# Small tiles of an encoder kernel padded or moved in SBUF

## The chip, the cores and the metric

The kernel runs on one core of one Trainium2 chip. The metric is the time of one execution on the device in microseconds (us); a smaller time is better. TensorE multiplies matrices (its weight loads are listed apart, as PEld), VectorE (DVE) and ScalarE (ACT) do elementwise work, GpSimd (POOL) does a few small operations, and SyncE (SP) issues the transfers from HBM. A core's working memory, SBUF, has 128 partitions; a tile takes the same bytes in each of them, so its place is one byte address within a partition.

## The reference, cut to what matters

The input x has 256 tokens of 2048 float32 values. Two layers follow each other. Each computes `x = LN(alpha*x + mixer(x))` and then `x = LN(alpha*x + SwiGLU(x))`.

- Layer 0's mixer is one projection of 2048 to 8192 columns, which feeds neighbourhood attention (8 heads) and a bidirectional gated recurrence (8 heads); their outputs, 2048 columns, go through an output projection of 2048 to 2048.
- Layer 1's mixer is a projection of 2048 to 2560 columns, which feeds multi-scale pooling and grouped-query attention, and again an output projection of 2048 to 2048.
- SwiGLU is `(silu(x @ w_gate) * (x @ w_up)) @ w_down` with a hidden width of 5632.

All data are float32. Nearly all of the arithmetic is the product of 256 tokens with these weight matrices.

## The kernel before

**Products.** A weight matrix is cut into pieces of 256 rows by 512 columns. One transfer brings a piece into the tile `raw` (line 139). It is split into two tiles, `whi` (a copy rounded to the fast matmul type, ACT, line 102) and `wlo` (the rest, DVE, line 103), each 4096 bytes a partition. Activations are split the same way into `xTh`/`xTl` or `yTh`/`yTl`. `mm3` (line 239) then makes each product from three matmuls: (whi, low activation), (whi, high), (wlo, high). The activation is the stationary operand, 128 by 128, loaded by LDWEIGHTS; the weight tile is the moving operand, 128 by 512, which streams through. A piece is 12 such matmuls: 2 token tiles, 2 row blocks, 3 parts. There are 760 pieces, so 9120 matmuls of 512 columns, all recorded at line 242. The other matmuls (attention, recurrence, transposes) move 128 or 256 columns.

**Where weight pieces lie.** `load_half` (line 123) takes the split tiles from rings of buffers in turn: `wp` has 6 buffers for `whi` and 6 for `wlo`. After layer 0's mixer, line 809 opens a second ring `wx` with 2, and lines 811 and 819 a third one, `f0` or `f1`, with 3 (called fp below). A newly opened ring is left alone for 12 pieces; then the pieces go round all rings, with 11 slots while fp is open and 8 slots during layer 1's mixer. So until the first `wx` piece, the 1705th of the 512-column matmuls, only `wp` is read; of the 7416 from there on, 4200 read `wp`, 1368 `wx` and 1848 fp (counted in the program: the trace holds the program's 10,180 matmuls in the program's order, so each matmul of the trace is matched to its buffers).

**Addresses.** Pools are laid out one behind the other in the order in which they are opened: `cp` (two constants), `wp`, `acts` (activations), `sm` (small tiles), and behind them `ab` (layer 0's mixer), or `res`, `wx`, and `f0`, `cd` or `f1`. Small tiles are rounded up to 32 bytes. The program's own list of addresses gives:

| tiles | first address | address modulo 256 |
|---|---|---|
| `ident`, 512 bytes | 1152 | 128 |
| `mhalf`, 32 bytes | 1664 | 128 |
| `raw`, `whi`, `wlo` of `wp` (each 4096 bytes) | 1696 | 160 |
| `xTh`, `xTl`, `yTh`, `yTl` (65,536 bytes in all) | 67232 | 160 |
| `sm`: 1344 bytes of small tiles | 132768 | 160 |
| all of `ab`: `qT`, `kT`, `pt`, `av`, `qq`, `kk`, ... | 134112 | 224 |
| `whi`, `wlo` of `wx` | 150496 | 224 |
| `gam`, `bet` (8192 bytes each), `betT` (64 bytes) | 166880 | 224 |
| `whi`, `wlo` of fp, behind `betT` | 183328 | 32 |
| `cc`, `sn`, `nwq`, `nwk`, `pscale` (32 bytes) of `cd` | 166880 | 224 |
| `rcount` and all that follows in `cd`: `band`, `dv`, `dkT`, `dqT`, `pt`, `cn`, `pw`, ... | 169984 | 0 |

**Order of the work.** The framework plans the order of each engine's instructions from the program and its priorities; loads and splits run ahead of the products by up to as many pieces as there are buffers. SP's queue holds the weight transfers in program order.

**Lines of the change.** `ident` and `mhalf` (lines 83 to 86) are made once on POOL; `mhalf` is the exponent -0.5 of `rstd_of` (line 199). `mv` (line 263) holds mean and variance in `norm`. `betT` (line 329) is a bias that `flip` reads. `pscale` (line 681) scales the pooling output.

Of the kernel before, what the change touches and what calls it, by code (L numbers as in the profile page):

```python
# [11 lines left out]
F32 = mybir.dt.float32  # L12
# [4 lines left out]
PSUM = bass.MemoryType.PSUM  # L17

P = 128
T = 256  # L20
NT = T // P
D = 2048
KT = D // P
# [14 lines left out]

# column blocks (units of 128) of the chunks of the first projection
A_Q, A_K, A_V, H_Q, H_FF, H_FB, H_I, H_G = (8 * i for i in range(8))  # L40
# [32 lines left out]
def trunk(ctx: ExitStack, tc: tile.TileContext, a, out):  # L73
    nc = tc.nc
# [6 lines left out]
    ps = ctx.enter_context(tc.tile_pool(name="ps", bufs=1, space=PSUM))  # L81

    ident = cp.tile([P, P], F32, name="ident")
    make_identity(nc, ident)
    mhalf = cp.tile([P, 8], F32, name="mhalf")
    nc.gpsimd.memset(mhalf, -0.5)

# [1 line left out]
    def acc():  # L89
# [14 lines left out]

    # a norm whose transposes go between the next products, one step a piece
    pending = []

    # pools with room for split weight pieces, taken in turn
    rings = [(wp, 6)]
    turn = [0]  # L110

    def open_ring(pool, bufs):
        # the first pieces keep to the older pools: the new one's memory may still be in use
        rings.append((pool, bufs))
        turn[0] = -12

    # instructions that the splits of the next pieces are queued behind
    ahead = []
    held = [0]
    last_load = [None]  # L120
    first = [True]
# [27 lines left out]
    def mm_chunk(halves, lhs, outs, tok_major=False, after=None, before=None):  # L149
        """outs[tok] += x[tok] @ w for the chunk; halves: (dram piece, first k tile)."""  # L150
        n = len(halves)
        loaded = []

        def step():
            if next(pending[0], None) is None:
                pending.pop()

        def mms(i, tok, pin=False):
            hi, lo = loaded[i]
            k0 = halves[i][1]  # L160
            for kk in range(2):
                xh, xl = lhs(tok, k0 + kk)
                first = i == 0 and kk == 0
                last = i == n - 1 and kk == 1
                mm3(outs[tok], (xh, xl), (hi[:, kk, :], lo[:, kk, :]), first, last, pin)

        if tok_major:
            for i, (src, _) in enumerate(halves):
                if pending and i >= FREE:
                    held[0] = 1  # L170
                loaded.append(load_half(src))
            for tok in range(NT):
                for i in range(n):
                    if pending and i >= FIRST_STEP:
                        step()
                    mms(i, tok, True)
                    if pending and tok == 0:
                        held[0] = HELD
                while pending:
                    step()  # L180
                if after:
                    after(tok)
        else:
            for i, (src, _) in enumerate(halves):
                loaded.append(load_half(src, before(i) if before else ()))
                for tok in range(NT):
                    mms(i, tok)
            if after:
                for tok in range(NT):
                    after(tok)  # L190

    def rstd_of(var, n, scale=None, eps=LN_EPS):
        """(var * scale + eps) ** -0.5, [P, n]"""
        r = sm.tile([P, 8], F32, tag="rstd", name="rstd", bufs=6)
        if scale is None:
            nc.vector.tensor_scalar(r[:, :n], var, eps, None, op0=add)  # L196
        else:
            nc.vector.tensor_scalar(r[:, :n], var, scale, eps, op0=mult, op1=add)
        nc.gpsimd.tensor_tensor(r[:, :n], r[:, :n], mhalf[:, :n], op=ALU.pow)  # L199
        return r  # L200

    # activations of the current projection, transposed and split, per token tile
    def new_xT():
# [19 lines left out]

    # transposes of src [P tok, 512] into the group's token slice, split
    def transpose4(src, hi, lo):
# [13 lines left out]
    def mm3(o, lhs, rhs, start, stop, pin=False):  # L239
        """o += lhs.T @ rhs, both as high and low parts"""  # L240
        for n, (a, b) in enumerate(((1, 0), (0, 0), (0, 1))):
            ins = nc.tensor.matmul(o, lhs[a], rhs[b], start=start and n == 0, stop=stop and n == 2)  # L242
            if pin:
                tc.keep_in_program_order(ins)
# [3 lines left out]

# [1 line left out]
    def residual_tools(res, gam, bet, betT):  # L250
# [11 lines left out]
        def norm(tok, xT=None, out_rows=None):  # L262
            mv = sm.tile([P, 2], F32, tag="mv", name="mv")
            nc.vector.bn_aggr(mv, stats[tok])
# [59 lines left out]
    def load_gb(pool, i, which):  # L324
        g = pool.tile([P, D], F32, tag="gam", name="gam", bufs=1)
        b = pool.tile([P, D], F32, tag="bet", name="bet", bufs=1)
        nc.sync.dma_start(g, a[f"ln_{which}_g"][i : i + 1, :].to_broadcast([P, D]))
        nc.sync.dma_start(b, a[f"ln_{which}_b"][i : i + 1, :].to_broadcast([P, D]))
        bT = pool.tile([P, KT], F32, tag="betT", name="betT", bufs=1)
        nc.sync.dma_start(bT, a[f"ln_{which}_bT"][i])  # L330
        return g, b, bT

# [1 line left out]
    def out_proj(w, order, groups, res, gb):  # L334
# [15 lines left out]

# [1 line left out]
    def ffn(fp, layer, xT, res, gb, last):  # L352
# [41 lines left out]

# [1 line left out]
    def attend(pool, probs, v_of):  # L396
        """o [d, h, q] = (probs[h] [q, k] v [k, d]).T in PSUM, for two heads"""
        pts = []
# [12 lines left out]
    def exp_rows(pool, src, nm):  # L411
        """softmax of src [P, NT, T] with the negated row maxima nm"""
        e = pool.tile([P, NT, T], F32, tag="e", name="e", bufs=2)
# [9 lines left out]
    def ab_mixer(mp, xT, yT):  # L423
        def load_x(i):
            """the part of x that goes with piece i of the first chunk"""
            if i % 2:
# [20 lines left out]
        def constants_in():  # L447
            first[0] = False
            with tc.issue_after(last_load[0]):
# [3 lines left out]
                nc.sync.dma_start(colmask, a["col_mask"])  # L453
            # lower bounds: cumulative softmax over the layers' logits, less its first
            nc.vector.tensor_tensor(ex, lg, lg, op=sub)
# [6 lines left out]
        lhs = x_lhs(xT)  # L462
# [15 lines left out]
        def pairT(t, col):  # L478
            """two heads at column col of t [tok, 512] -> psum [d, 2, T]"""
            q = trp().rearrange("p (h t) -> p h t", h=2)  # L480
            for h in range(2):
                for tok in range(NT):
                    transpose(
                        q[:, h, tok * P : (tok + 1) * P], t[:, tok, col + h * P : col + (h + 1) * P], ident
                    )
            return q
# [17 lines left out]
        def hgq(i, outs):  # L504
# [15 lines left out]
            nc.gpsimd.memset(Qb, 1.0)  # L520
            # att[s, 0, h, st, t]: blocks on the diagonal; [s, 1, ...]: off it
            att = mp.tile([P, 2, 4, P], F32, tag="att", name="att", bufs=1)
# [146 lines left out]

# [1 line left out]
    def cd_mixer(mp, xT, yT):  # L671
# [8 lines left out]
        nc.vector.tensor_scalar(nw["q"], nw["q"], QSCALE, None, op0=mult)  # L680
        pscale = mp.tile([P, 8], F32, name="pscale", bufs=1)
        nc.sync.dma_start(pscale, a["pool_scale"])
# [12 lines left out]
        def normed(src, nh, w, tok):  # L695
            """rms norm and rotary positions of src [tok, nh, 128] in PSUM"""
            ss = sm.tile([P, 4], F32, tag="ss", name="ss")
# [101 lines left out]

# [1 line left out]
    xT = new_xT()  # L801
# [21 lines left out]

# [1 line left out]
def constants():  # L825
# [10 lines left out]
    for g, w in enumerate(POOL_WINDOWS):  # L836
        lo, hi = np.clip(pos - w // 2, 0, T), np.clip(pos + w // 2, 0, T)
        for t in range(T):
            # windows cut short are summed here and divided later; the others' divisors are powers of two
            n = hi[t] - lo[t]  # L840
# [23 lines left out]

# [1 line left out]
def pieces(w, blocks=None):  # L866
    """[K, N] -> [N/512, K/256, 128, 2, 512], columns in the order of the blocks of 128"""
    k, n = w.shape
# [62 lines left out]
```

## Time and profile before

| | |
|---|---|
| time of the runs | 2254.0, 2255.23, 2255.7 us; median 2255.23 us |
| span of the profiled execution | 2252.3 us |
| TensorE matmul / weight load, busy | 2225.6 us (99%) / 1834.7 us (81%) |
| VectorE / ScalarE / GpSimd, busy | 1314.7 (58%) / 992.2 (44%) / 78.9 us (4%) |
| chain of waits that ended last | 96% TensorE; 91% the products of line 242 into `acc` |

The span runs from the first to the last instruction; the page has no other time for the profiled execution, and the median of the timed runs is 2.9 us above its span. A matmul's row in the timeline has its start and its length. Matmuls are pipelined, so the length (about 0.39 us) is not the pace; the pace is the distance from one start to the next.

### The profile page before, as it was taken

Reading aid. Unit: us, or ns where it says so; the run is one execution under the profiler, and the core shown is the slowest. Engines: PE = TensorE matmul, PEld = TensorE weight load, DVE = VectorE, ACT = ScalarE, POOL = GpSimd, SP = SyncE. Lnnn points to the kernel's source line nnn. Section 1 sums busy time; section 2 is a strip of 40 time slices with the busy share of each in tenths; the row PEclk is TensorE's granted clock in tenths of the full one; section 3 lists DMA queues with packets and bytes.
Section 4 is the critical chain, followed back from the end, with each engine's and each line's share of the span. In section 5 each row is a group of like instructions: output and inputs, shape, how many; then the busy total and the mean of one; then the engine's idle time right before and its main releaser. Section 6 shows DMA issues by size and latency. Waiting matters only on the chain.

```text
span 2252.3 us, 26810 instructions
## 1 busy us (share of the span) xinstructions
PE 2225.6 (99%) x10180; PEld 1834.7 (81%) x10180; DVE 1314.7 (58%) x1662; ACT 992.2 (44%) x1258; POOL 78.9 (4%) x67
## 2 busy tenths in 40 slices
PE   8999999999999999999999999999999999999997
PEld 7888888887888888888888788878888888888886
DVE  6886687567555444544555676665454554544454
ACT  6445544446443444334443555444434444344431
POOL 0010001002000000000000200020000000000000
PEclk9999999999999999999999999999999999999999
DMA  8555545666555656555555464746555555556551
GB/s 291 159 159 185 171 134 184 225 225 231 180 196 180 201 179 196 176 199 184 193 176 194 151 203 132 243 158 224 193 188 189 178 196 178 199 176 201 181 196 66
DMA packets 118897, 420.65 MB, mean 187 GB/s; under 512 B 14448, under 2 KB 17008, under 8 KB 117488
## 3 DMA queue, kind: packets, MB, share of 16 engines
q1 hardware_dynamic: 118768, 418.94, 56.4%
q8 instruction: 80, 1.31, 0.2%
q14 instruction: 49, 0.40, 0.1%
HBM read 416.78 MB, written 2.10 MB: 186 GB/s over the span
## 4 chain that ended last, share of the span: by engine, by line
PE 96%; DVE 2%; ACT 1%; DMA 1%; issue 0%; POOL 0%; SPq 0%; DVEq 0%; ACTq 0%; POOLq 0%
PE acc L242 91%; PE tr L99 2%; PE mx L529 1%; DVE wlo L103 1%; PE mx L242 1%; DMA raw<-in_cd_in 0%; PE mx L575 0%; PE mx L782 0%; ACT res L287 0%; ACT whi L102 0%; DVE xTl L318 0%; DMA raw<-in_ab_in 0%; DVE res L273 0%; DVE res L277 0%; PE mx L765 0%
## 5 line engine op out<-in xcount | busy, mean ns | idle before, releaser
L103 DVE TENSOR_TENSOR wlo<-raw,whi 128x1024 fp32r<-128x1024 f32 (+1 forms) x761 | 939.4, 1237 | 743.2 <-ACT whi L102 734.0
L102 ACT CAST whi<-raw 128x1024 fp32r<-128x1024 f32 (+1 forms) x761 | 797.8, 1050 | 1009.9 <-PE acc L242 828.1
L242 PE MATMUL acc<-whi,xTl 128*128 128x512 f32 x2080 | 819.8, 396 | 13.7 <-DVE xTl L318 8.0
L242 PE MATMUL acc<-whi,xTh 128*128 128x512 f32 x2080 | 818.7, 394 | 0.0
L242 PE MATMUL acc<-wlo,xTh 128*128 128x512 f32 x2080 | 813.5, 394 | 0.3 <-DVE wlo L103 0.3
L242 PEld LDWEIGHTS acc<-whi,xTl 128*128 128x128 f32 x2080 | 392.5, 189 | 98.2 <-DVE xTl L318 8.5
L242 PEld LDWEIGHTS acc<-wlo,xTh 128*128 128x128 f32 x2080 | 392.2, 189 | 86.8 <-DVE wlo L103 0.7
L242 PEld LDWEIGHTS acc<-whi,xTh 128*128 128x128 f32 x2080 | 392.6, 189 | 83.0
L242 PE MATMUL acc<-whi,yTl 128*128 128x512 f32 x960 | 377.8, 394 | 0.1
L242 PE MATMUL acc<-whi,yTh 128*128 128x512 f32 x960 | 376.5, 392 | 0.0
L242 PE MATMUL acc<-wlo,yTh 128*128 128x512 f32 x960 | 372.8, 392 | 0.0
L242 PEld LDWEIGHTS acc<-wlo,yTh 128*128 128x128 f32 x960 | 180.3, 188 | 40.6 <-DVE wlo L103 0.4
L242 PEld LDWEIGHTS acc<-whi,yTl 128*128 128x128 f32 x960 | 180.4, 188 | 39.7 <-DVE yTl L788 0.3
L242 PEld LDWEIGHTS acc<-whi,yTh 128*128 128x128 f32 x960 | 180.3, 188 | 39.6
L199 POOL TENSOR_TENSOR rstd<-rstd,mhalf 128x4 f32<-128x4 f32 (+2 forms) x18 | 17.5, 974 | 1828.4 <-DVE rstd L196 1678.7
L103 DVE TENSOR_TENSOR yTl<-tr,yTh 128x512 fp32r<-128x512 f32 x48 | 31.1, 686 | 81.5 <-ACT yTh L102 81.5
L102 ACT CAST yTh<-tr 128x512 fp32r<-128x512 f32 x48 | 26.0, 590 | 96.4 <-PE tr L99 96.3
L319 POOL TENSOR_TENSOR res<-res,bet 128x512 f32<-128x512 f32 x24 | 39.2, 1638 | 27.2 <-PE tr L99 14.5
L258 DVE TENSOR_TENSOR res<-res,acc 128x512 f32<-128x512 f32 x32 | 21.9, 684 | 27.2 <-PE acc L242 26.2
L529 PEld LDWEIGHTS mx<-qq,kk 128*128 128x128 f32 x256 | 33.6, 191 | 2.6
L529 PE MATMUL mx<-qq,kk 128*128 128x128 f32 x256 | 33.8, 274 | 0.0
L256 DVE SCALAR_TENSOR_TENSOR res<-res,acc 128x512 f32<-128x512 f32 x32 | 21.7, 682 | 17.1 <-PE acc L242 16.8
(162 smaller groups left out, 825.9 us busy)
## 6 DMA issues: line engine op xcount, KB each, us to landing
raw<-in_gate SPq DMA_DIRECT2D x176, 512.0 KB, 4.3
raw<-in_up SPq DMA_DIRECT2D x176, 512.0 KB, 4.1
raw<-in_down SPq DMA_DIRECT2D x176, 512.0 KB, 4.2
raw<-in_ab_in SPq DMA_DIRECT2D x127, 512.0 KB, 4.2
raw<-in_cd_in SPq DMA_DIRECT2D x40, 512.0 KB, 4.3
raw<-in_ab_out SPq DMA_DIRECT2D x32, 512.0 KB, 4.6
raw<-in_cd_out SPq DMA_DIRECT2D x32, 512.0 KB, 4.2
x<-in_xT SPq DMA_DIRECT2D x8, 256.0 KB, 6.1
```

What stands on the lines that cost most here:

```text
L99: return nc.tensor.transpose(o, src, eye)
L102: nc.scalar.copy(hi, src)
L103: nc.vector.tensor_tensor(lo, src, hi.bitcast(F32), op=sub)
L199: nc.gpsimd.tensor_tensor(r[:, :n], r[:, :n], mhalf[:, :n], op=ALU.pow)
L242: ins = nc.tensor.matmul(o, lhs[a], rhs[b], start=start and n == 0, stop=stop and n == 2)
L256: nc.vector.scalar_tensor_tensor(r, r, ALPHA, psum, op0=mult, op1=add)
L258: nc.vector.tensor_tensor(r, r, psum, op=add)
L319: nc.gpsimd.tensor_tensor(r, r, bet[:, s], op=add)
L529: nc.tensor.matmul(m[:, 2 * h + s, :], kk[:, h, s * P : (s + 1) * P], qq[:, h, r * P : (r + 1) * P], start=True, stop=True,)
```

## The change

`mhalf` is padded from 32 to 128 bytes and placed ahead of `ident`, as the first tile of the pool `cp`. `mv` has 2 buffers instead of 4 (64 bytes less in `sm`). `betT` and `pscale` are padded to 256 bytes. Each padded tile is used through a slice of its old size. Comments and doc strings are dropped as well.

```diff
+    mhalf = cp.tile([P, 32], F32, name="mhalf")[:, :8]
+    nc.gpsimd.memset(mhalf, -0.5)
     ident = cp.tile([P, P], F32, name="ident")
     make_identity(nc, ident)
-    mhalf = cp.tile([P, 8], F32, name="mhalf")
-    nc.gpsimd.memset(mhalf, -0.5)
...
-            mv = sm.tile([P, 2], F32, tag="mv", name="mv")
+            mv = sm.tile([P, 2], F32, tag="mv", name="mv", bufs=2)
...
-        bT = pool.tile([P, KT], F32, tag="betT", name="betT", bufs=1)
+        bT = pool.tile([P, 64], F32, tag="betT", name="betT", bufs=1)[:, :KT]
...
-        pscale = mp.tile([P, 8], F32, name="pscale", bufs=1)
+        pscale = mp.tile([P, 64], F32, name="pscale", bufs=1)[:, :8]
```

## Rows read from the trace of the kernel before

**Rows 1.** The page: its first line, the busy times of its part 1, and the shares by engine of part 4, the chain of work that ended last.

```profile
span 2252.3 us, 26810 instructions
...
PE 2225.6 (99%) x10180; PEld 1834.7 (81%) x10180; DVE 1314.7 (58%) x1662; ACT 992.2 (44%) x1258; POOL 78.9 (4%) x67
...
PE 96%; DVE 2%; ACT 1%; DMA 1%; issue 0%; POOL 0%; SPq 0%; DVEq 0%; ACTq 0%; POOLq 0%
```

**Rows 2.** Waits of TensorE, longest first: who was waited for, us in total, times, the longest.

```profile
PE acc L242 <- DVE xTl L318: 8.0, 2, 4.0
PE acc L242 <- DVE xTl L103: 5.6, 1, 5.6
PE tr L99 <- ACT res L287: 1.3, 1, 1.3
PE acc L242 <- DVE wlo L103: 0.3, 1, 0.3
```

**Rows 3.** The chain of waits in order of time, merged: start us, us, what, and how many instructions. The first two rows are stretches of layer 0's mixer, the others of the two SwiGLU stages.

```profile
36.72 19.74 PE acc L242 x87
...
241.82 22.24 PE acc L242 x98
...
570.52 44.14 PE acc L242 x192
...
660.55 110.46 PE acc L242 x480
...
907.01 132.57 PE acc L242 x576
...
1642.13 110.45 PE acc L242 x480
...
2157.18 83.83 PE acc L242 x364
```

**Rows 4.** Timeline of TensorE in layer 0's mixer: the first rows of two pieces in `wp`, with 11 matmuls of the same kind left out between them (start us, length us, engine, line, operation).

```profile
127.54 0.39 PE L242 MATMUL acc<-whi,xTl 128*128 128x512 f32 x1
...
130.26 0.39 PE L242 MATMUL acc<-whi,xTl 128*128 128x512 f32 x1
```

**Rows 5.** Timeline of TensorE in layer 0's SwiGLU: the first rows of consecutive pieces, 11 matmuls left out after each. The pieces lie in `wp` (868.28), `wx` (871.00), fp (873.77), `wp` (876.56) and `wp` (879.33); of the later ones the piece at 893.09 lies in fp and the ones at 890.37, 895.88 and 898.62 in `wp`.

```profile
868.28 0.39 PE L242 MATMUL acc<-whi,xTl 128*128 128x512 f32 x1
...
871.00 0.40 PE L242 MATMUL acc<-whi,xTl 128*128 128x512 f32 x1
...
873.77 0.40 PE L242 MATMUL acc<-whi,xTl 128*128 128x512 f32 x1
...
876.56 0.39 PE L242 MATMUL acc<-whi,xTl 128*128 128x512 f32 x1
...
879.33 0.39 PE L242 MATMUL acc<-whi,xTl 128*128 128x512 f32 x1
...
890.37 0.39 PE L242 MATMUL acc<-whi,xTl 128*128 128x512 f32 x1
...
893.09 0.40 PE L242 MATMUL acc<-whi,xTl 128*128 128x512 f32 x1
...
895.88 0.39 PE L242 MATMUL acc<-whi,xTl 128*128 128x512 f32 x1
...
898.62 0.39 PE L242 MATMUL acc<-whi,xTl 128*128 128x512 f32 x1
```

**Rows 6.** Timeline of TensorE, matmuls of 256 columns in the attention: two rows of layer 0 (3 matmuls left out between them), two of layer 1 (20 left out).

```profile
223.28 0.28 PE L242 MATMUL mx<-kTh,qTh 128*128 128x256 f32 x1
...
223.76 0.28 PE L242 MATMUL mx<-kTl,qTh 128*128 128x256 f32 x1
...
1341.88 0.28 PE L242 MATMUL mx<-dkTh,dqTl 128*128 128x256 f32 x1
...
1344.40 0.28 PE L242 MATMUL mx<-dkTl,dqTh 128*128 128x256 f32 x1
```

**Rows 7.** Timeline of TensorE in layer 0's mixer, where 8 small matmuls come between those of a piece: the small ones, the first matmul after them, and three later rows (6 and 2 matmuls left out before the last two).

```profile
133.20 1.05 PE L529 MATMUL mx<-qq,kk 128*128 128x128 f32 x8
134.01 0.48 PE L242 MATMUL acc<-whi,xTh 128*128 128x512 f32 x1
134.33 0.39 PE L242 MATMUL acc<-wlo,xTh 128*128 128x512 f32 x1
...
135.94 0.39 PE L242 MATMUL acc<-whi,xTl 128*128 128x512 f32 x1
...
136.62 0.39 PE L242 MATMUL acc<-whi,xTl 128*128 128x512 f32 x1
```

**Rows 8.** Busy time by engine from 870 to 1260 us (layer 0's SwiGLU): stretch, length, then PE, PEld, DVE, ACT and POOL busy with their instructions, the granted TensorE clock, the share of the DMA engines, GB/s.

```profile
870.00:1260.00 390.00, 390.00 (x1724) 319.01 (x1723) 195.76 (x188) 156.24 (x166) 4.07 (x4) 1.00 0.56 183
```

**Rows 9.** The instructions that the edits touch: POOL's, by group (with count, busy us, mean ns, idle before); VectorE's write of `mv` and the first read of `ident`, by tile (count, shortest, median and longest in ns, first and last start).

```profile
masks.py:199 POOL TENSOR_SCALAR_AFFINE_SELECT ident<-ident 128x128 f32<-128x128 f32 x1 | 0.3, 292 | 0.0
masks.py:197 POOL MEMSET ident<- 128x128 f32 x1 | 0.2, 204 | 0.3 <-POOLq L927 0.3
L86 POOL MEMSET mhalf<- 128x8 f32 x1 | 0.1, 104 | 0.0
...
L264 DVE BATCH_NORM_AGGREGATE mv<-st x8: 252/262/265, 502.1 to 2242.5; 128x2 f32<-128x24 f32 x8
...
L99 PEld LDWEIGHTS tr<-ident,nat x64: 138/140/143, 31.8 to 399.6; 128*128 128x128 f32 x64
```

## The prediction

> **What bounds the kernel now.** I read the page first: TensorE is busy for 99% of the span and holds 96% of the chain that ended last [rows 1]. The list of its waits comes next: they add up to about 15 us [rows 2], so nothing that feeds TensorE can be worth more than that. What counts is how fast TensorE runs through its own queue, and that isn't in the busy time but in the distance between starts. The third view is therefore the chain in order of time, in which long unbroken stretches of products carry their count [rows 3]. Length over count is the pace. In layer 0's mixer it is 19.74/87 = 226.9 ns and 22.24/98 = 226.9 ns for a matmul of 512 columns. In the SwiGLU stages it is 44.14/192 = 229.9, 110.46/480 = 230.1, 132.57/576 = 230.2, and near the end 83.83/364 = 230.3 ns. [...]
>
> The fourth view, the timeline, shows where. Twelve matmuls of a `wp` piece in the mixer take 130.26 - 127.54 = 2.72 us, 226.7 ns each [rows 4]. In SwiGLU pieces of several rings follow each other [rows 5]: a `wp` piece again 226.7 ns (868.28 to 871.00), a `wx` piece 2.77/12 = 230.8, an fp piece 2.79/12 = 232.5, the `wp` piece behind it 2.77/12 = 230.8. The fp piece at 893.09 takes 232.5, the `wp` piece behind that 228.3. So a ring has its own pace, and a `wp` piece behind another ring's needs some matmuls to get back to 226.7.
>
> What differs between the rings is the address. The stationary tiles lie at 160 modulo 256. `wp` lies at 160 too, `wx` at 224, fp at 32. My reading is that TensorE's moving read and its weight load disturb each other unless both start at the same place in a 256-byte period. [...] That it is the relative place, and not 160 itself, I take from the 256-column matmuls, whose two operands come from one pool: at 224 and 224, 0.48/4 = 120 ns; at 0 and 0, 2.52/21 = 120 ns [rows 6]. [...]
>
> **The change part by part.** *Addresses.* `mhalf` takes bytes 1152 to 1280, `ident` starts at 1280 = 5 x 256, `wp` at 1792 = 7 x 256; `wp`, its `raw` tiles and `acts` are whole multiples of 256. `sm` falls from 1344 to 1280 bytes, so what follows starts at 134144 = 524 x 256. With `betT` at 256 bytes fp starts at 183552 = 717 x 256, and with `pscale` padded the rest of `cd` stays at 0. Every moving and stationary tile is at 0, as only the 256-column matmuls of layer 1 are now.
>
> *What it gives.* 7416 matmuls come after the first `wx` piece. At 230.0 ns (middle of the four values above) against 226.9, the pace of uninterrupted stretches that read `wp` alone, they lose 7416 x 3.1 = 23.0 us. Two things keep this from being more. The first 1704 are already in step and gain nothing. And after small matmuls TensorE loses step whatever the ring: from 134.33 to 135.94 seven matmuls take 1.61 us, 230 ns each, and then three take 0.68, 226.7 again [rows 7]. That is 0.02 us for each return; the 226.9 of [rows 3] contains one return in each stretch, and the trace has 68 returns after the first `wx` piece, 1.6 us or so in all, that I let stand.
>
> *What it costs.* The `mhalf` memset of 104 ns is now ahead of `ident`, whose two instructions take 0.50 us; the first transpose reads `ident` at 31.8 us [rows 9], so 31 us cover 0.1. Without the cover it would be 0.1 us. `mv` with 2 buffers: the write for the third norm half waits for the reads of the first, on VectorE itself or one ScalarE pass earlier, a stage before; there are 8 such writes of 262 ns in 1740 us [rows 9]. I take 0; if each wait cost as much as the longest wait of TensorE on a norm, 4.0 us [rows 2], six would be 24 us, but queued behind the write is only the norm it belongs to, and the tile it waits for has long been read. Padded `betT` and `pscale` change no instruction's element count: 0. The engines that feed TensorE must keep up with 1.3% more pace; they are at 50% (DVE), 40% (ACT) and 56% (DMA) in that stage [rows 8], so what is late next is still TensorE. What the trace does not show is the pace of 512-column matmuls with both operands at 0. Bounds from both sides: 226.7 ns as at 160 and 160 [rows 4], or the 232.5 of the worst ring [rows 5], by which all 9120 would lose 2.5 x 9120 = 23 us against now. I take 226.7, since 256-column matmuls run alike at 0 and at 224.
>
> The sum: 2252.3 - 23.0 = 2229.3 us of span; the runs' median is 2.9 above the span, so 2232.
>
> [...]
>
> **The rivals.**
> - *The period is 512, not 256.* Modulo 512 `wp` and `acts` will be at 256, fp at 256, but `wx` (150528) at 0. Then fp falls into step and `wx` does not. For it: before, the offsets from the stationary tile are 64 (`wx`) and 128 (fp) modulo 256, and nothing in the trace has an offset of 256. Against it: nothing. It leaves 1368 x (230.8 - 226.7) = 5.6 us, and at each of the 176 places where TensorE comes from `wx` to another ring up to 12 x 4.1 = 0.05 us of getting back (0.02 at the least, by the piece at 895.88): 4 to 9 us. The gain is about 11 us: 2244.
> - *The ring's place in memory sets the pace.* `wx` and fp lie at 150 KB and above, `wp` and `acts` below 133 KB; distance might matter and the low address bits not. For it: ring and region always go together in these rows. Against it: the 256-column matmuls in step lie above 178 KB, moving and stationary alike. Then nothing changes: 2255. A planner that orders the work otherwise, with no gain, comes out here too.
> - *Slower: both operands at 0 get in each other's way.* If a 512-column matmul never falls into step when both reads start at the beginning of a period, every one of the 9120 stays at the pace of getting back, 230 ns at the least [rows 7], up to fp's 232.5. It decides at 229.5 ns, today's mean over both parts: (1704 x 227.6 + 7416 x 230.0)/9120, with 227.6 for the mixer: 226.7 and the 0.02 us of 78 returns. At 231.3, the middle, it costs 9120 x 1.8 = 16 us: 2271. For it: those 256-column matmuls are few, and short streams may hide it. Against it: 21 of them in a row at 120 ns [rows 6].
> - *The returns go as well.* If the loss after small matmuls comes from `ident` at 128 or the mixer's tiles at 224 beside 160, it disappears too: another 1.6 us and some 2 us in the mixer, 2228.
>
> **How the numbers follow.** All in step: 0.60 (with the last rival inside it, 0.10 of these). Period 512: 0.18. No change: 0.12. Slower: 0.08. Something else, either way: 0.02. Predicted: 2232. The range of 2227 to 2246 takes in the first two, and the case without returns at its low end; no change, slower and the rest, 0.22, are outside. A difference of 0.2% (4.5 us) is about what a measurement can tell from none. Faster by more than that: 0.60 + 0.18 + 0.01 = 0.79; within: 0.12; slower: 0.09.
>
> **What would show it.** Right: in the chain the stretches of 192 products fall from 44.14 to about 43.55 us and those of 576 from 132.57 to 130.6; the mixer's x98 stays at 22.24; all pieces of the timeline, whatever the ring, take 2.72 us once in step; the 256-column rows stay at 120 ns. Period 512: `wx` pieces alone stay above 2.75 us. Region: all stays. Slower: the mixer's x98 rises to 22.5 or more. Wrong altogether: the pace falls as forecast and the span does not, with a new wait of TensorE in the list, on `xTl` or `wlo` above all.

## The result, and the profile after

The changed kernel takes 2230.8 us (median of 4 runs, 2229.76 to 2232.15) against 2254.61 us for the kernel before (4 runs, the three listed above and a fourth of 2254.0 us): a ratio of 0.9894, 95% interval 0.988 to 0.9908, 1.1% faster. The forecast was 2232, the range 2227 to 2246. One run of the kernel before, among those beside the experiments, was slow at 5260.81 us and enters no ratio.

The page of the changed kernel, the lines that answer to [rows 1]. Line numbers are one higher than before.

```profile
span 2228.0 us, 26810 instructions
...
PE 2201.6 (99%) x10180; PEld 1833.9 (82%) x10180; DVE 1313.6 (59%) x1662; ACT 994.5 (45%) x1258; POOL 83.1 (4%) x67
...
PE 96%; DVE 2%; ACT 1%; DMA 0%; issue 0%; POOL 0%; DVEq 0%; ACTq 0%; POOLq 0%
```

TensorE lost 24.0 us of busy time with the same 10,180 matmuls, and the span fell by 24.3. VectorE and ScalarE worked as long as before, within 0.3%; GpSimd, at 4% of the span, 4 us longer. TensorE's waits, the answer to [rows 2], did not move:

```profile
PE acc L243 <- DVE xTl L319: 8.0, 2, 4.0
PE acc L243 <- DVE xTl L104: 5.7, 1, 5.7
PE tr L100 <- ACT res L288: 1.0, 1, 1.0
PE acc L243 <- DVE wlo L104: 0.3, 1, 0.3
```

So the time came from the pace. The chain in order of time (start us, us, what, how many), the answer to [rows 3]:

```profile
36.38 19.74 PE acc L243 x87
...
241.14 22.23 PE acc L243 x98
...
568.49 43.55 PE acc L243 x192
...
657.34 108.85 PE acc L243 x480
...
900.34 130.61 PE acc L243 x576
...
1626.41 108.82 PE acc L243 x480
...
2134.17 82.54 PE acc L243 x364
```

The two stretches of layer 0's mixer take what they took. Every stretch of the SwiGLU stages is now at the mixer's pace: 43.55/192 = 226.8 ns, 130.61/576 = 226.8 ns. The timeline, the answer to [rows 5], shows four pieces in a row, in `wp`, `wx`, fp and `wp`, and the start of the next (first rows, 11 matmuls left out after each):

```profile
862.80 0.39 PE L243 MATMUL acc<-whi,xTl 128*128 128x512 f32 x1
...
865.52 0.39 PE L243 MATMUL acc<-whi,xTl 128*128 128x512 f32 x1
...
868.24 0.39 PE L243 MATMUL acc<-whi,xTl 128*128 128x512 f32 x1
...
870.96 0.39 PE L243 MATMUL acc<-whi,xTl 128*128 128x512 f32 x1
...
873.68 0.39 PE L243 MATMUL acc<-whi,xTl 128*128 128x512 f32 x1
```

Each takes 2.72 us, 226.7 ns for a matmul, the pace that is called in step here. Where the rings differed and a piece behind another ring's was slow, nothing differs now.

With each matmul matched to its buffers, as in the section on the kernel before, the mean distance between starts in ns is as follows. It is taken from the first `wx` piece on, and distances over 270 ns, in front of small matmuls or behind a pause, are left out.

| | `wp` | `wx` | fp | loss against 226.67 ns, all rings |
|---|---|---|---|---|
| before | 228.61 | 230.96 | 232.60 | 24.7 us |
| after | 226.89 | 226.96 | 226.85 | 1.7 us |

In the part ahead of the first `wx` piece the loss went from 2.1 to 1.6 us. These distances hold 23.5 of the 24.3 us by which the span fell; where the other 0.8 us went was not followed.

### The profile page after: what moved, and what is told of

Its sections match the earlier page's. It is cut to its first block, busy times and chain, and to the rows that moved or that the text cites. A ratio compares the mean times of both kernels' runs of the same rounds, so it can differ in the third digit from the quotient of the medians.

```text
span 2228.0 us, 26810 instructions
## 1 busy us (share of the span) xinstructions
PE 2201.6 (99%) x10180; PEld 1833.9 (82%) x10180; DVE 1313.6 (59%) x1662; ACT 994.5 (45%) x1258; POOL 83.1 (4%) x67
## 4 chain that ended last, share of the span: by engine, by line
PE 96%; DVE 2%; ACT 1%; DMA 0%; issue 0%; POOL 0%; DVEq 0%; ACTq 0%; POOLq 0%
PE acc L243 91%; PE tr L100 2%; PE mx L530 1%; PE mx L243 1%; DVE wlo L104 1%; DVE xTl L319 0%; PE mx L576 0%; PE mx L783 0%; ACT whi L103 0%; ACT res L288 0%; DVE res L274 0%; DMA raw<-in_cd_in 0%; DMA x<-in_xT 0%; DVE res L278 0%; PE mx L766 0%
```

## The experiments

The question was why the pace follows the addresses. Three theories stood against each other: only the places of the two reads relative to each other count (R, mine); a multiple of 256 itself counts (M); the ring's place in memory counts (P). Others came up on the way.

**All tiles at 160 modulo 256.** 160 more bytes in front of everything, and room made by leaving `pscale` unpadded:

```diff
-    mhalf = cp.tile([P, 32], F32, name="mhalf")[:, :8]
+    mhalf = cp.tile([P, 72], F32, name="mhalf")[:, :8]
...
-        pscale = mp.tile([P, 64], F32, name="pscale", bufs=1)[:, :8]
+        pscale = mp.tile([P, 8], F32, name="pscale", bufs=1)
```

> The changed kernel with 160 more bytes in front (mhalf 288 bytes) and pscale unpadded: moving and stationary tiles of every 512-column matmul start at 160 modulo 256, none at a multiple of 256. Theory R (only the place of the two reads relative to each other counts): as the changed kernel, 2231 us, stretches of 192 products 43.55 us. Rival M (a multiple of 256 itself counts): no tile has it, so it loses all that the change gave, 2254 us or more, 44.1 us for 192. Rival P (the ring's place in memory counts, and the change helped by another way): 2254 us, with fp and wx pieces slow and wp pieces at 226.7 ns.

Measured: 2231.34 us (4 runs), a ratio of 0.9892 to the kernel before, interval 0.9875 to 0.991. Its chain:

```profile
243.14 22.23 PE acc L243 x98
...
571.51 43.55 PE acc L243 x192
```

No tile that the products read begins at a multiple of 256, and the kernel is as fast as the changed one. M falls: what the change's edits do is right, but not because of 256-byte starts. What they gave is one common remainder.

**The stationary tiles moved away from the rings.** Seven kernels, each run once, shift all activations `xT` and `yT` against the three rings by one offset, and give the rest of a period back behind them. Here for 128:

```diff
+    sm.tile([P, 32], F32, name="rest", bufs=1)
...
-    mhalf = cp.tile([P, 32], F32, name="mhalf")[:, :8]
+    mhalf = cp.tile([P, 24], F32, name="mhalf")[:, :8]
...
+    ap_.tile([P, 32], F32, name="skew", bufs=1)
...
-        pscale = mp.tile([P, 64], F32, name="pscale", bufs=1)[:, :8]
+        pscale = mp.tile([P, 8], F32, name="pscale", bufs=1)
```

> The changed kernel with all rings at 224 modulo 256 and all stationary activations 128 bytes further (96 modulo 256): every 512-column matmul has the offset that fp pieces had before, whose mean distance was 232.6 ns. Theory R: all 9120 go to about 232.6 ns from 227.0, 9120 x 5.6 = 51 us more: span 2279 us, x192 stretches 44.6 us, wp as slow as fp. Rival P: wp pieces stay at 226.7 ns; span 2228 to 2252 us. Rival V (only where the moving tile starts counts): all rings alike, but no more than the 231.0 ns that wx pieces at 224 had: 2264 us.

> The same with the stationary activations 192 bytes further than the rings (160 and 224 modulo 256): the offset and the two places that wx pieces had before, mean distance 231.0 ns. Theory R: all 9120 at about 231.0 ns, 36 us more: span 2264 us, and a difference to off128 of some 15 us. Rival V: the same time as off128, since the moving tiles start at 224 in both. Rival P: 2228 to 2252 us.

> The same with an offset of 32 bytes (224 and 0 modulo 256), which neither kernel had. Theory R: out of step too, between 228 and 233 ns, span 2237 to 2283 us; if the two reads meet in units of 64 bytes, as at offset 0: 2228 us. Rival V: as off128 and off192.

The chain of off128, then of off192, then of off32:

```profile
246.25 22.78 PE acc L245 x98
...
579.92 44.61 PE acc L245 x192
```

```profile
244.15 22.45 PE acc L245 x98
...
574.48 43.96 PE acc L245 x192
```

```profile
247.28 22.85 PE acc L245 x98
...
581.58 44.80 PE acc L245 x192
```

The spans are 2277.9, 2248.0 and 2284.9 us. With the offset that only fp had before, all 9120 matmuls go at 232.5 ns, the mixer's, which read `wp` alone, too: x98 rises from 22.23 to 22.78 us. R's 2279 holds to 1 us, and P falls, since `wp` lies where it lay (at 18 KB to 67 KB) and is as slow as fp. V, that only the moving tile's start counts, falls as well: the rings are at 224 in all three, and the times differ by up to 37 us. For off192 R's number was wrong by 16 us: I had taken the 231.0 ns of `wx` before for its own pace. When all rings share the offset, the pace is 229.0. The other 2 ns were the way into it, from pieces of other rings: before the change the first four distances of a `wx` stretch were 233.6 ns on average, those from the fifth on 228.4.

The other four offsets, to see the law:

> Offset 64 bytes (moving tiles at 224, stationary ones at 32 modulo 256). Measured so far, span by offset: 0 2228.0 and 2231.7, 32 2284.9, 128 2277.9, 192 2248.0 us. Theory R with a smooth dependence on the offset: between the neighbours, 2278 to 2285 us. Rival S (the same loss for an offset and its opposite, 64 and 192): 2248 us.

> Offset 96 bytes. Theory R, smooth: 2278 to 2285 us. Rival S gives no number here (160 is not measured).

> Offset 160 bytes. Theory R, smooth: between 128 and 192, 2248 to 2278 us. Rival S: as offset 96.

> Offset 224 bytes, that is 32 below a whole period. Theory R, smooth and falling from 32 to 256: between 192 and 0, 2228 to 2248 us; an offset better than 0 would show here, below 2227 us. Rival S: as offset 32, 2285 us.

| offset, bytes | span us | one stretch x192, us | mean ns |
|---|---|---|---|
| 0 (changed kernel) | 2228.0 | 43.55 | 227.0 |
| 32 | 2284.9 | 44.80 | 233.3 |
| 64 | 2286.3 | 44.80 | 233.3 |
| 96 | 2293.0 | 44.98 | 234.2 |
| 128 | 2277.9 | 44.61 | 232.5 |
| 160 | 2287.2 | 44.80 | 233.3 |
| 192 | 2248.0 | 43.96 | 229.0 |
| 224 | 2285.2 | 44.80 | 233.3 |

All four smooth forecasts missed, by 1 us at 64, by 8 at 96, by 9 at 160 and by 37 at 224. S holds for 32 and 224 but not for 64 and 192, and 96 and 160 are 6 us apart. No law came out. There is no slope towards 0: 32 bytes to either side cost 57 us, as much as most offsets. 0 is the best of the eight.

**Which read disturbs which.** In the changed kernel a weight load starts right behind the start of a matmul and loads for the next one (timeline, TensorE and its weight loads):

```profile
870.05 0.39 PE L243 MATMUL acc<-wlo,xTh 128*128 128x512 f32 x1
870.06 0.19 PEld L243 LDWEIGHTS acc<-whi,xTl 128*128 128x128 f32 x1
...
870.28 0.39 PE L243 MATMUL acc<-whi,xTl 128*128 128x512 f32 x1
870.28 0.19 PEld L243 LDWEIGHTS acc<-whi,xTh 128*128 128x128 f32 x1
```

So I put only `xTl` off, with a skew of 128 bytes between `xTh` and `xTl` (rings and `xTh` are at 224 modulo 256, `xTl` at 96, and `yTh` and `yTl`, behind it, too; the room is made as above):

```diff
+    skewed = []
+
     def new_xT():
         xh = [ap_.tile([P, KT, P], F32R, tag=f"xTh{t}", name=f"xTh{t}") for t in range(NT)]
+        if not skewed:
+            skewed.append(ap_.tile([P, 32], F32, name="skew", bufs=1))
         xl = [ap_.tile([P, KT, P], F32R, tag=f"xTl{t}", name=f"xTl{t}") for t in range(NT)]
```

> High activations xTh in step with the rings, low activations xTl 128 bytes off (and yTh, yTl too). Of three matmuls of an x product, (whi, xTl), (whi, xTh), (wlo, xTh), the weight load of xTl runs beside the stream of (wlo, xTh) before it. Theory L (the load disturbs the stream that it runs beside): starts are late behind (wlo, xTh) alone, 232.5 against 226.7 ns, mean 228.6; span 2228 + 6240 x 1.9 ns + 2880 x 5.6 ns = 2256 us. Rival O (a matmul is disturbed by its own weights' place): late behind (whi, xTl) alone, the same span. Rival K (one misfit in three keeps all out of step, since getting back takes some six matmuls): 230 ns or more everywhere, 2265 us or more.

Measured: span 2271.3 us (one run), 15 more than L and O gave. From the timeline, and the lengths of two groups of weight loads (count, shortest, median and longest in ns, first and last start):

```profile
880.63 0.40 PE L248 MATMUL acc<-wlo,xTh 128*128 128x512 f32 x1
880.87 0.40 PE L248 MATMUL acc<-whi,xTl 128*128 128x512 f32 x1
881.10 0.39 PE L248 MATMUL acc<-whi,xTh 128*128 128x512 f32 x1
...
882.71 0.40 PE L248 MATMUL acc<-wlo,xTh 128*128 128x512 f32 x1
```

```profile
L248 PEld LDWEIGHTS acc<-whi,xTl x2080: 187/188/330, 5.5 to 2168.6; 128*128 128x128 f32 x190
L248 PEld LDWEIGHTS acc<-whi,xTh x2080: 187/192/333, 5.7 to 2168.8; 128*128 128x128 f32 x190
```

Nine distances, 880.63 to 882.71, take 231.1 ns each. Over the whole kernel, and finer than these rows' 0.01 us, the mean distance behind (wlo, xTh) is 232.2 ns, behind (whi, xTl) 234.2, behind (whi, xTh) 227.4. Each of the three theories fails on a part. L is right that the stream beside which the misfit is loaded is late; that one differs from an undisturbed matmul in nothing but the load beside it, so the load does disturb the stream. The misfit's load itself is no longer than in the changed kernel, 188 ns in the median of both, so the next start does not wait for a longer load. But the next one, in whose time a fitting tile is loaded, is late as well. The third is normal, so it isn't K either: one misfit spoils two matmuls, not all. With these values the x products lose 6240 x (231.3 - 227.0) = 27 us and the y products 2880 x 5.4 = 16, in all the 43 us measured. Why the second is late stays open; the fitting load in its time takes 192 ns, 4 more than in the changed kernel.

**One part at a time.** Put fp off by 128 or `wx` by 192, as before the change, and leave the rest in step:

```diff
-        bT = pool.tile([P, 64], F32, tag="betT", name="betT", bufs=1)[:, :KT]
+        bT = pool.tile([P, 32], F32, tag="betT", name="betT", bufs=1)[:, :KT]
```

> The changed kernel with betT padded to 128 bytes instead of 256: the rings of fp start at 128 modulo 256, as far from the stationary tiles as before the change; all else is in step. Theory R: 1848 fp matmuls lose 5.6 ns (10.3 us), and behind each of the 227 fp stretches another ring's matmuls need some 0.03 us to get back in step (7 us): 2231 + 17 = 2248 us, wx pieces at 226.7 ns once in step. Rival (no loss behind a ring that is out of step): 2241 us.

```diff
-            mv = sm.tile([P, 2], F32, tag="mv", name="mv", bufs=2)
+            mv = sm.tile([P, 2], F32, tag="mv", name="mv", bufs=4)
...
-        bT = pool.tile([P, 64], F32, tag="betT", name="betT", bufs=1)[:, :KT]
+        bT = pool.tile([P, 48], F32, tag="betT", name="betT", bufs=1)[:, :KT]
...
-        pscale = mp.tile([P, 64], F32, name="pscale", bufs=1)[:, :8]
+        pscale = mp.tile([P, 48], F32, name="pscale", bufs=1)[:, :8]
```

> The changed kernel with mv at 4 buffers, betT at 192 and pscale at 192 bytes: wx starts at 64 modulo 256, as far from the stationary tiles as before the change; wp and fp are in step. Theory R: 1368 wx matmuls lose 4 ns (5.4 us), and behind each of the 176 wx stretches 0.02 to 0.03 us (3.5 to 5 us): 2240 to 2242 us. Rival: the offset of 192 costs 2.0 ns when every ring has it (off192), so 2.7 us and nothing behind it: 2234 us.

Measured: fp128 2245.2 us, ratio 0.9954 (0.9937 to 0.9971); wx64 2244.0 us, 0.995 (0.9935 to 0.9965). Against the changed kernel's 2230.8, fp out of step costs 14.4 us and `wx` 13.2. Together that is more than the 23.8 us that the change gave, but by no more than the intervals allow. The distances are finer: over the changed kernel's 3.3 us the loss is 13.3 and 12.9 us, together 26.2, and with both rings out of step, before the change, it is 23.5. A ring that is out of step also costs the one behind it, and the two share those places. By ring, in ns from the first `wx` piece on:

| | `wp` | `wx` | fp | loss in all, us |
|---|---|---|---|---|
| changed kernel | 226.89 | 226.96 | 226.85 | 3.3 |
| fp128 | 227.67 | 226.99 | 232.34 | 16.6 |
| wx64 | 227.42 | 231.08 | 229.39 | 16.2 |

For fp128 the forecast was 3 us too high: fp's own loss is 1830 x 5.5 = 10.0 us as forecast, what comes behind it 3.2 instead of 7. For wx64 it was 2 to 4 us too low, and its rival by 10: 155 of the 176 `wx` stretches are followed by fp, and fp, itself in step, averages 229.39.

**An offset of 16 bytes.** This asks whether the two reads share units of 32 bytes, the smallest step so far. The activations get 64 columns of padding and start 4 columns in; `raw` gives up a buffer for the room:

```diff
+    def skewed(n, **kw):
+        t = ap_.tile([P, n + 64], F32R, **kw)
+        return t[:, 4 : 4 + n]
...
-            raw = wp.tile([P, 2, NCH], F32, tag="raw", name="raw", bufs=4)
+            raw = wp.tile([P, 2, NCH], F32, tag="raw", name="raw", bufs=3)
...
-        yh = ap_.tile([P, 4, T], F32R, tag="yTh", name="yTh", bufs=4)
+        yh = skewed(4 * T, tag="yTh", name="yTh", bufs=4).rearrange("p (k t) -> p k t", k=4)
```

> Stationary activations 16 bytes off the rings (0 and 16 modulo 256); room for it comes from raw, which has 3 buffers instead of 4. The offsets of 32 and 224, one step to either side of 0, both cost 57 us of span (2284.9 and 2285.2). Theory U (the two reads share units of 32 bytes or more): in step as at offset 0, x192 stretches 43.55 us, span 2228 to 2232 us with what the missing raw buffer may cost. Theory B (every displacement of the start counts): out of step, 233 ns or so, x192 stretches near 44.8 us, span 2285 us. [...]

Its chain from 560 us on:

```profile
579.01 0.87 PE tr L105 x8
579.89 43.53 PE acc L248 x192
623.42 0.87 PE tr L105 x8
624.29 44.80 PE acc L248 x192
669.09 0.87 PE tr L105 x8
```

Neither theory expected this: both happen. The same work, with all tiles at the same remainders, takes 43.53 us in one stretch and 44.80 in the next. Of the 30 stretches of 60 or more matmuls between small ones, 8 stay at 226.7 ns after their first dozen matmuls, 21 at 233.3, and one lies between. A stretch keeps the pace with which it came out of the small matmuls: in the one at 579.89 the distances behind the first are 227 and 226 ns, in the one at 624.29 they are 236 and 234. This is what "in step" looks like: a state that holds itself. At offset 0 every stretch finds it, at 16 some do, and at 32 the mean of 233.3 leaves no room for it. The span of 2283.9 us also holds what the missing buffer of `raw` costs, which I did not measure apart; TensorE's waits add up to 24.3 us in it, against 15.0 in the changed kernel.

## Why the prediction was right

**The bound.** Right. Nothing that feeds TensorE became late; the waits are those of before, with the engines at 51% (DVE), 41% (ACT) and 57% (DMA) in SwiGLU:

```profile
863.00:1248.00 385.00, 385.00 (x1726) 319.23 (x1725) 195.96 (x187) 156.94 (x168) 3.76 (x4) 1.00 0.57 186
```

The granted clock was 1.00 in this stage as in [rows 8], and in the kernel before also in layer 0's mixer, so it explains neither the pace that was lost nor the one that came back:

```profile
100.00:461.00 361.00, 361.00 (x1837) 306.06 (x1836) 260.15 (x462) 171.45 (x261) 19.82 (x16) 1.00 0.56 178
```

**The cause.** Right. That the relative place of the moving read and the weight load counts, and not 160 itself, was taken from 256-column matmuls alone [rows 6]. It is shown now by all160, where both are at 160, and by the offsets, where one is moved. The period is not 512: in the changed kernel `wx` lies 256 bytes off modulo 512, the first rival's case, and is in step. It is not 128 either, as off128 shows. The prediction had no row on the first of these, and its 0.18 for that rival said so. Layer 0's 256-column matmuls went from 224 to 0 and stay at 120 ns (10 left out):

```profile
221.80 0.28 PE L243 MATMUL mx<-kTh,qTl 128*128 128x256 f32 x1
...
223.12 0.28 PE L243 MATMUL mx<-kTl,qTh 128*128 128x256 f32 x1
```

How the two reads get in each other's way, no run shows. What is measured is that the same load beside the same stream costs nothing or 2 to 7 ns by its address: 227.0 ns on average at offset 0, 229.0 to 234.2 at the seven others.

**The sum.** 7416 x 3.1 = 23.0 us was forecast for the part from the first `wx` piece on; the losses there fell from 24.7 to 1.7 us, by 23.0. That this agrees to 0.1 us is partly luck: 230.0 was the middle of four values, and their ends, 229.9 and 230.3, give 22.2 and 25.2 us. The 226.9 ns of the mixer's stretches were the right floor, as the returns after small matmuls stayed: the forecast let 1.6 us of them stand, and 1.7 us are left there. The rows of [rows 7] in the changed kernel:

```profile
132.67 1.05 PE L530 MATMUL mx<-qq,kk 128*128 128x128 f32 x8
133.48 0.48 PE L243 MATMUL acc<-whi,xTh 128*128 128x512 f32 x1
133.79 0.40 PE L243 MATMUL acc<-wlo,xTh 128*128 128x512 f32 x1
...
134.48 0.39 PE L243 MATMUL acc<-wlo,xTh 128*128 128x512 f32 x1
...
135.16 0.39 PE L243 MATMUL acc<-wlo,xTh 128*128 128x512 f32 x1
```

Three matmuls at 0.69/3 = 230 ns and then 226.7, where it was seven before. A little of the last rival came true: in the mixer the loss fell by 0.5 us. Most of it stayed, although every tile that TensorE reads, `ident` and those of the small matmuls too, is at 0 now, so these addresses are not what makes TensorE lose step.

**The costs.** Zero, as forecast. The `mhalf` memset, now ahead of `ident`, is 0.1 us:

```profile
masks.py:197 POOL MEMSET ident<- 128x128 f32 x1 | 0.2, 205 | 0.0
L85 POOL MEMSET mhalf<- 128x8 f32 x1 | 0.1, 105 | 0.3 <-POOLq L928 0.3
```

No wait on a norm grew, so two buffers of `mv` are enough.

**The slower rival**, that a 512-column matmul with both operands at 0 doesn't fall into step, had its test in the mixer's x98: 22.23 us, not the 22.5 it needed.

**What the prediction did not size.** The sum holds for both rings together and gives no price for one alone. Only the first rival had one for `wx`: 5.6 us of its own and 4 to 9 behind it, a time of 2244. wx64, with `wx` at its old offset, measured 2244.0; of the 12.9 us lost, 1346 x (231.08 - 226.96) = 5.5 us are its own and 7.4 lie with the rings behind it.

## What to carry to other kernels

When the engine that bounds a kernel is busy all the time, read its pace from starts over counts, stage by stage, and compare the same instruction in two stages: 1.4% here (226.9 against 230.1 ns) was hidden under "busy 99%". For a stream of matmuls whose weights are loaded one ahead, give moving and stationary tiles the same remainder modulo 256 bytes; which one didn't matter here (2230.8 us at 0, 2231.34 at 160), and padding a few small tiles in front does it. Six of the seven offsets in steps of 32 bytes cost 50 to 65 us, 2 to 3% of this kernel, so it is worth looking at the allocation whenever a small tile is added. Shown is this for one type and shape, weight loads of 128 by 128 and moving tiles of 512 columns in float32, on one core.

## What the runs showed that was not expected

- The pace has states that hold themselves: at an offset of 16 bytes equal stretches take 43.53 or 44.80 us, and which of the two shows within the first few distances.
- Losses don't shrink towards offset 0: 32 bytes off costs 57 us, 192 only 20.
- Half the columns take more than half the time: in step, starts of 512-column matmuls are 226.7 ns apart, at a common remainder of 0 as at 160, and those of the 256-column ones of [rows 6] 120 ns. By these two paces, as an estimate, a column takes (226.7 - 120)/256 = 0.417 ns, and 226.7 - 512 x 0.417 = 13 ns, the time of some 32 columns, come on top. No steady stretch here comes below 226.7, and no run shows what this time is for.
